# A hybrid decoder trunk on one core: the order of the long and the short product in the feed-forward blocks

## The chip, the cores and the metric

The kernel runs on one core of one Trainium2 chip. Its time is the device time of that core in microseconds (us), from launch to end; the profile's span is the time from the first to the last recorded instruction. The time before is 2571.78 us, the median of three runs (2567.96 to 2573.69).

## What is computed

Two layers of a decoder trunk over 256 tokens of width 2048, all in float32. Each layer has a modulation by a condition vector, head groups (gated DeltaNet and sliding-window attention) between an input and an output projection, and a SwiGLU feed-forward of inner width 5632. The change lies in the feed-forward alone:

```python
h = rms_norm(x, ln_ffn[l]) * (1.0 + sc_f) + sh_f
gate, up = jnp.split(h @ w_gate_up[l], 2, axis=-1)      # 2048 -> 2 x 5632
x = x + gt_f * ((jax.nn.silu(gate) * up) @ w_down[l])   # 5632 -> 2048
```

## The kernel before

The token axis is kept whole: an activation tile is 128 features by 256 tokens, and weights are the stationary operand of TensorE in blocks of 128x128. To keep float32 accuracy at the faster fp32r rate, each weight block w is split into a rounded part wh (a cast on ScalarE, ACT) and a remainder wl (a subtraction on VectorE, DVE, or in the projections partly on GpSimd, POOL). Each activation is split in the same way into a tile `a` of 128 x 2 x 256: `a[:, 0, :]` is the rounded part, written by ACT, and `a[:, 1, :]` the remainder, written by DVE. A product keeps three terms: wh with both parts of the activation, and wl with the rounded part.

In the projections (`mm3`) these are three products of 256 columns. In the feed-forwards (`mm2`, line 725) the two terms with wh are merged into one product of 512 columns, which fills a whole accumulation bank; the term with wl is a product of 256 columns onto the bank's first half. The two halves are added when the bank is emptied (`swiglu` for gate and up, `add_x` for down). A block is one weight block with one activation tile, so two products: here "long" for 512 columns, "short" for 256. Every product has a weight load of its own in the instruction stream.

Who calls `mm2`:
- `gemm_pair` (line 753): one gate block row and one up block row, 16 blocks each, into the two banks of one tile `pr`. 42 of the 44 pairs of a layer.
- `pair_quad` (line 779) through `quad`: the first two pairs of a layer, four accumulations side by side, because the activations are still being made (`make` in `normed`): for each k, four blocks go to four banks.
- `gemm_two` (line 746): the down projection, 22 blocks into one bank `psm`, for 16 output tiles and two halves of the inner width. The first eight of the 22 activations lie in a tile named `mid`, the rest in `act`.

In all, a layer has 44 x 2 x 16 = 1408 blocks of gate and up and 2 x 16 x 22 = 704 of down; with two layers 4224 blocks.

The order of everything is set while the program is recorded: a planner (`Steps`, `Timed`) keeps an estimated clock for each engine and lets small steps of other work, splits of coming weights (`Weights.split`, four blocks at a time) and transfers be issued between blocks (`S.tick()` in `into`, line 732). TensorE's estimate for a product depends on its form and columns. Transfers go out on one queue, that of SyncE (SP).

Of the kernel before, what the change touches and what calls it, by code (L numbers as in the profile page):

```python
# [26 lines left out]
D, T, L, H, NH, FT = 2048, 256, 2, 8, 16, 44  # L27
# [406 lines left out]
def trunk(tc, xT, bada, c, c_col, par, con, w_in, w_ba, w_ada0, w_ada, w_out, w_gu, w_dn, out):  # L434
    nc = Timed(tc.nc)
    with (
# [244 lines left out]
        first, na, nw = [], 0, 0  # L681
# [36 lines left out]
        def mm3(q, w, a, first, last):  # L718
# [3 lines left out]
            nc.tensor.matmul(q, wl, a[:, 0, :], start=False, stop=last)  # L722
            nc.floor = 0

        def mm2(q, w, a, first, last):

            wh, wl, nc.floor = w
            nc.tensor.matmul(q, wh, a.rearrange("p a c -> p (a c)"), start=first, stop=False)
            nc.tensor.matmul(q[:, 0:T], wl, a[:, 0, :], start=False, stop=last)
            nc.floor = 0  # L730

        def into(q, mm, acts, lo, hi):
# [13 lines left out]
        def gemm_two(acts, lo=0, hi=None, tag="pm"):  # L746

            S.grab(b, tag)
            q = b.bank(tag)
            into(q, mm2, acts, lo, len(acts) if hi is None else hi)  # L750
            return Held(q, lambda: b.give(tag))

        def gemm_pair(acts):

            S.grab(b, "pr")
            q = b.bank("pr")
            for i in range(2):
                into(q[:, i * 512 : i * 512 + 512], mm2, acts, 0, KT)
            return Held(q, lambda: b.give("pr"))
# [19 lines left out]
        def pair_quad(make):  # L779
            for _ in range(2):  # L780
                S.grab(b, "pr")
            qs = [Held(b.bank("pr"), lambda: b.give("pr")) for _ in range(2)]
            quad(mm2, [q.ap[:, i * 512 : i * 512 + 512] for q in qs for i in range(2)], make)
            return qs
# [960 lines left out]
```

## Time and profile before

| | |
|---|---|
| median of three runs | 2571.78 us (2567.96 to 2573.69) |
| the profiled execution's own time | 2571.36 us |
| its span | 2569.6 us |
| mean granted TensorE clock | 0.98 |
| products on TensorE (each with a load) | 16878 |
| HBM read | 603.44 MB |

How to read the profile: engines are PE (TensorE's products), PEld (its weight loads, which overlap PE), DVE, ACT, POOL and SP. A row of a group names line, engine, operation, the tiles (output <- inputs), shapes and count, then busy time in us, mean ns of one, and the engine's idle time just before with what ended it. Line 172 is the helper through which every operation is recorded, so groups are told apart by their tiles: `pr` is the accumulation of gate and up, `psm` that of down, of small work and of some projections, `pm` that of the projections. A row of the timeline is start, duration, engine, operation and tiles; PE's products overlap, since each begins while the one before it drains, so the distance between two starts is what a product costs, not its duration. Tile `act` or `mid` is the activation, `wh` and `wl` the weight's parts. PE's ends are modelled.

### The profile page before, as it was taken

What the parts mean: (1) busy time and instruction counts of PE and PEld (TensorE: products, weight loads), DVE (VectorE), ACT (ScalarE), POOL (GpSimd) and SP (SyncE); (2) the same over time, 40 slices, a digit from 0 to 9 for tenths busy, and PEclk for the clock granted to TensorE, in tenths of its full rate; (3) what the DMA queues carried; (4) which work ended last, traced back from release to release, by engine and by line L of the source; (5) the groups of instructions that cost most, each with busy time, mean ns of one, the idle gap of its engine ahead of it and who ended that gap; (6) DMA issues with size and microseconds to landing.
All of it is one profiled execution on the core that took longest, in us unless ns stands there. A gap on an engine that the chain in (4) does not pass through costs nothing.

```text
span 2569.6 us, 46036 instructions
## 1 busy us (share of the span) xinstructions
PE 2462.8 (96%) x16878; PEld 2174.5 (85%) x16878; DVE 1854.1 (72%) x3823; ACT 1294.3 (50%) x2760; POOL 432.7 (17%) x389
## 2 busy tenths in 40 slices
PE   6999898988999999999999999899899999999998
PEld 4887786987888888888888899899788888888887
DVE  3758767787667999999987876655877655555665
ACT  4346553535545445555445655454555544555553
POOL 1433232670000000000004333246000000000000
PEclk9999998998999999999999999899999999999999
DMA  9987575776777999999984443346677766555564
GB/s 353 338 302 255 194 244 181 249 272 199 244 245 268 341 354 347 352 345 344 328 299 132 133 131 126 118 161 225 214 253 246 243 187 191 189 183 195 180 185 137
DMA packets 192789, 609.08 MB, mean 237 GB/s; under 512 B 27825, under 2 KB 39217, under 8 KB 192561
## 3 DMA queue, kind: packets, MB, share of 16 engines
q1 hardware_dynamic: 192562, 606.14, 68.9%
q8 instruction: 132, 2.16, 0.3%
q14 instruction: 95, 0.78, 0.1%
HBM read 603.44 MB, written 2.10 MB: 236 GB/s over the span
## 4 chain that ended last, share of the span: by engine, by line
PE 52%; issue 32%; DVE 9%; DMA 3%; ACT 2%; POOL 1%; SPq 1%; DVEq 0%; POOLq 0%; ACTq 0%
PE psm L172 19%; PE pr L172 18%; PE pm L172 15%; DMA wada<-w_ada 3%; DVE wl L172 2%; ACT wh L172 1%; DVE wada L172 1%; POOL wl L172 1%; DVE act L172 1%; DVE cv L172 1%; DVE R L172 1%; DVE x L172 1%; DMA wx<-w_ada 0%; SPq L121 0%; DVE ry L172 0%
## 5 line engine op out<-in xcount | busy, mean ns | idle before, releaser
L172 ACT CAST wh<-w 128x512 fp32r<-128x512 f32 x1532 | 894.2, 604 | 456.7 <-PE psm L172 177.0
L172 DVE TENSOR_TENSOR wl<-w,wh 128x512 fp32r<-128x512 f32 (+1 forms) x1293 | 860.3, 683 | 243.7 <-ACT wh L172 234.4
L172 PE MATMUL pr<-act,wh 128*128 128x512 f32 x2816 | 994.7, 395 | 7.3 <-DVE kq L172 4.0
L172 PE MATMUL pr<-act,wl 128*128 128x256 f32 x2816 | 799.0, 284 | 0.0
L172 PE MATMUL pm<-act,wh 128*128 128x256 f32 x3328 | 641.4, 292 | 14.0 <-DVE x L172 4.1
L172 PEld LDWEIGHTS pr<-act,wh 128*128 128x128 f32 x2816 | 531.7, 189 | 132.3 <-DVE act L172 4.7
L172 PEld LDWEIGHTS pm<-act,wh 128*128 128x128 f32 x3328 | 519.0, 192 | 36.3 <-issue 21.2
L172 PEld LDWEIGHTS pr<-act,wl 128*128 128x128 f32 x2816 | 532.2, 189 | 0.0
L172 POOL TENSOR_TENSOR wl<-w,wh 128x512 fp32r<-128x512 f32 (+1 forms) x239 | 331.0, 1395 | 1190.9 <-PE psm L172 762.5
L172 PE MATMUL pm<-act,wl 128*128 128x256 f32 x1664 | 473.3, 284 | 1.4 <-POOL wl L172 1.4
L172 DVE CUSTOM_DVE_ANT_0 wada<-wada,cs 128x1024 f32<-128x1024 f32 x256 | 331.8, 1296 | 129.0 <-DMA wada<-w_ada 128.8
L172 PE MATMUL psm<-act,wh 128*128 128x512 f32 (+1 forms) x1280 | 390.8, 362 | 2.4 <-DVE act L172 2.1
L172 PEld LDWEIGHTS pm<-act,wl 128*128 128x128 f32 x1664 | 318.6, 191 | 2.3 <-POOL wl L172 2.2
L172 PE MATMUL psm<-act,wl 128*128 128x256 f32 x1088 | 308.3, 283 | 0.0
L172 PEld LDWEIGHTS psm<-act,wh 128*128 128x128 f32 x1280 | 228.3, 189 | 46.0 <-issue 6.1
L172 PEld LDWEIGHTS psm<-act,wl 128*128 128x128 f32 x1088 | 205.2, 189 | 0.0
L172 PE MATMUL psm<-mid,wh 128*128 128x512 f32 x512 | 183.4, 396 | 0.0
L172 PE MATMUL psm<-mid,wl 128*128 128x256 f32 x512 | 144.1, 281 | 0.0
L172 POOL TENSOR_TENSOR n2r<-ms,halfc 128x2 f32<-128x2 f32 x5 | 3.5, 690 | 803.5 <-DVE ms L172 803.5
L172 ACT COPY kq<-pr 128x512 f32<-128x512 f32 x88 | 51.6, 587 | 169.3 <-PE pr L172 169.1
L172 PEld LDWEIGHTS psm<-mid,wh 128*128 128x128 f32 x512 | 96.1, 188 | 22.8
L172 DVE TENSOR_TENSOR kq<-pr,kq 128x512 f32<-128x512 f32 x88 | 60.5, 687 | 72.9 <-ACT kq L172 72.9
(188 smaller groups left out, 1957.9 us busy)
## 6 DMA issues: line engine op xcount, KB each, us to landing
w<-w_gu SPq DMA_DIRECT2D x352, 512.0 KB
wada<-w_ada SPq DMA_DIRECT2D x320, 512.0 KB
w<-w_in SPq DMA_DIRECT2D x130, 512.0 KB
w<-w_dn SPq DMA_DIRECT2D x128, 512.0 KB
wx<-w_ada SPq DMA_DIRECT2D x64, 512.0 KB
w<-w_out SPq DMA_DIRECT2D x64, 512.0 KB
w<-w_dn SPq DMA_DIRECT2D x64, 384.0 KB
w<-w_in SPq DMA_DIRECT2D x28, 384.0 KB
```

Source lines behind the costliest of these rows:

```text
L172: return f(*a, **k)
```

## The change

A flag `turn` is kept across the calls of `mm2`. The first block of an accumulation sets it to 0; each later call flips it. Where it is 0 the block has the order of before, long then short. Where it is 1 the short product comes first. The flag that ends an accumulation is set on whichever product is last.

```diff
+        turn = [0]
+
         def mm2(q, w, a, first, last):
 
+
             wh, wl, nc.floor = w
-            nc.tensor.matmul(q, wh, a.rearrange("p a c -> p (a c)"), start=first, stop=False)
-            nc.tensor.matmul(q[:, 0:T], wl, a[:, 0, :], start=False, stop=last)
+            turn[0] = 0 if first else 1 - turn[0]
+            if turn[0]:
+                nc.tensor.matmul(q[:, 0:T], wl, a[:, 0, :], start=False, stop=False)
+            nc.tensor.matmul(q, wh, a.rearrange("p a c -> p (a c)"), start=first, stop=last and turn[0] > 0)
+            if not turn[0]:
+                nc.tensor.matmul(q[:, 0:T], wl, a[:, 0, :], start=False, stop=last)
             nc.floor = 0
```

On PE, in the middle of a gate-and-up accumulation of layer 0, these rows stood in a row before (output <- activation, weight part, columns last; numbers tell the buffers apart):

```order
L172 MATMUL pr_1996_8960<-act_1725_7765,wh_1985_8908 128x512
L172 MATMUL pr_1996_8960<-act_1725_7765,wl_1986_8909 128x256
L172 MATMUL pr_1996_8960<-act_1730_7784,wh_1985_8908 128x512
L172 MATMUL pr_1996_8960<-act_1730_7784,wl_1986_8909 128x256
L172 MATMUL pr_1996_8960<-act_1734_7801,wh_1985_8908 128x512
L172 MATMUL pr_1996_8960<-act_1734_7801,wl_1986_8909 128x256
L172 MATMUL pr_1996_8960<-act_1739_7820,wh_1985_8908 128x512
L172 MATMUL pr_1996_8960<-act_1739_7820,wl_1986_8909 128x256
```

and these stand there now:

```order
L172 MATMUL pr_1996_8960<-act_1725_7765,wh_1985_8908 128x512
L172 MATMUL pr_1996_8960<-act_1725_7765,wl_1986_8909 128x256
L172 MATMUL pr_1996_8960<-act_1730_7784,wl_1986_8909 128x256
L172 MATMUL pr_1996_8960<-act_1730_7784,wh_1985_8908 128x512
L172 MATMUL pr_1996_8960<-act_1734_7801,wh_1985_8908 128x512
L172 MATMUL pr_1996_8960<-act_1734_7801,wl_1986_8909 128x256
L172 MATMUL pr_1996_8960<-act_1739_7820,wl_1986_8909 128x256
L172 MATMUL pr_1996_8960<-act_1739_7820,wh_1985_8908 128x512
```

Long and short alternated; now two short ones and two long ones follow each other, with two different activations and, inside a pair, two different weight blocks of the same split.

On PE, at the end of one down accumulation and the beginning of the next, before:

```order
L172 MATMUL psm_3311_14781<-act_3258_14557,wh_3312_14784 128x512
L172 MATMUL psm_3311_14781<-act_3258_14557,wl_3313_14785 128x256
L172 MATMUL psm_3311_14781<-act_3285_14671,wh_3312_14784 128x512
L172 MATMUL psm_3311_14781<-act_3285_14671,wl_3313_14785 128x256
L172 MATMUL psm_3331_14869<-mid_2674_11995,wh_3315_14800 128x512
L172 MATMUL psm_3331_14869<-mid_2674_11995,wl_3316_14801 128x256
L172 MATMUL psm_3331_14869<-mid_2706_12135,wh_3315_14800 128x512
L172 MATMUL psm_3331_14869<-mid_2706_12135,wl_3316_14801 128x256
```

and now:

```order
L172 MATMUL psm_3311_14781<-act_3258_14557,wh_3312_14784 128x512
L172 MATMUL psm_3311_14781<-act_3258_14557,wl_3313_14785 128x256
L172 MATMUL psm_3311_14781<-act_3285_14671,wl_3313_14785 128x256
L172 MATMUL psm_3311_14781<-act_3285_14671,wh_3312_14784 128x512
L172 MATMUL psm_3331_14869<-mid_2674_11995,wh_3315_14800 128x512
L172 MATMUL psm_3331_14869<-mid_2674_11995,wl_3316_14801 128x256
L172 MATMUL psm_3331_14869<-mid_2706_12135,wl_3316_14801 128x256
L172 MATMUL psm_3331_14869<-mid_2706_12135,wh_3315_14800 128x512
```

Since a count of blocks is even and the first block keeps its order, an accumulation now ends with a long product and the next begins with one, so the pairs go on across the boundary, with the output tile changing inside a pair.

On PE, at the first units of a feed-forward (`pair_quad`), where four blocks share one activation that has just been made, the difference shows the waits (semaphores of the engine named) that the moved products carry:

```order
 L172 MATMUL pr_1707_7694<-act_1710_7699,wl_1690_7625 128x256
+L172 MATMUL pr_1706_7693<-act_1712_7712,wl_1680_7567 128x256 [waits Activation_49]
 L172 MATMUL pr_1706_7693<-act_1712_7712,wh_1679_7566 128x512 [waits DVE_49]
-L172 MATMUL pr_1706_7693<-act_1712_7712,wl_1680_7567 128x256
 L172 MATMUL pr_1706_7693<-act_1712_7712,wh_1682_7585 128x512
 L172 MATMUL pr_1706_7693<-act_1712_7712,wl_1683_7586 128x256
+L172 MATMUL pr_1707_7694<-act_1712_7712,wl_1688_7608 128x256
 L172 MATMUL pr_1707_7694<-act_1712_7712,wh_1687_7607 128x512
-L172 MATMUL pr_1707_7694<-act_1712_7712,wl_1688_7608 128x256
```

There the short product of the first block has moved ahead and waits for ACT alone, and the long one behind it waits for DVE as it did; of four blocks the first and the third have changed places of their products, so pairs arise here too.

## The prediction

> **What bounds the kernel now.** I read the page's busy shares and its chain first, then the chain in order of time inside the feed-forwards, then the sum by stretches, and last single products.
>
> ```profile
> span 2569.6 us, 46036 instructions
> PE 2462.8 (96%) x16878; PEld 2174.5 (85%) x16878; DVE 1854.1 (72%) x3823; ACT 1294.3 (50%) x2760; POOL 432.7 (17%) x389
> PE 52%; issue 32%; DVE 9%; DMA 3%; ACT 2%; POOL 1%; SPq 1%; DVEq 0%; POOLq 0%; ACTq 0%
> ```
>
> PE is busy for 96% of the span, so the question is what sets the spacing of its products. The chain names PE for 52% and "issue" for 32%; this "issue" is one stretch, and the windows show what it hides.
>
> ```profile
> 487.00 21.72 PE pm L172 x183
> 853.45 116.58 PE psm L172 x662
> 970.02 247.19 PE pr L172 x1408
> 1805.90 752.49 issue
> ...
> 970.00:1217.00 247.00, 247.00 (x1409) 216.44 (x1408) 225.61 (x427) 127.11 (x238) 0.00 (x0) 1.00 0.97 346
> 1814.00:2555.00 741.00, 738.99 (x4208) 647.09 (x4208) 476.51 (x841) 379.44 (x709) 0.00 (x0) 1.00 0.62 203
> ```
>
> A chain row is start, length, work. A window row is: stretch, length, busy time of PE, PEld, DVE, ACT and POOL with counts, granted clock, DMA share, GB/s. In layer 0 the chain runs over 1408 products without a step to another engine. The "issue" stretch is the feed-forward of layer 1: its window has PE busy 738.99 of 741.00 us with 4208 products, so it is the same dense stream. Spacing of products is therefore the whole bill: 247.19 / 1408 = 175.56 ns a product, 351.1 ns a block (one 512-column and one 256-column product), and 738.99 / 4208 = 175.6 in layer 1, the same. In the projections, where every product has 256 columns, 21.72 / 183 = 118.7 ns.
>
> How many blocks the change touches is in the groups by form:
>
> ```profile
> L172 PE MATMUL pr<-act,wh 128*128 128x512 f32 x2816 | 994.7, 395 | 7.3 <-DVE kq L172 4.0 <-DVE act L172 3.3
> L172 PE MATMUL psm<-act,wh 128*128 128x512 f32 x896 | 317.2, 393 | 1.9 <-DVE act L172 1.6 <-DVE mod L172 0.2
> L172 PE MATMUL psm<-mid,wh 128*128 128x512 f32 x512 | 183.4, 396 | 0.0
> ```
>
> 2816 + 896 + 512 = 4224 blocks, 4224 x 351.1 ns = 1483 us, 58% of the span. The mean durations (395 ns) are latencies that overlap, so I work with distances between starts:
>
> ```profile
> 1000.06 0.39 PE L172 MATMUL pr<-act,wh 128*128 128x512 f32 x1
> 1000.29 0.28 PE L172 MATMUL pr<-act,wl 128*128 128x256 f32 x1
> 1000.41 0.40 PE L172 MATMUL pr<-act,wh 128*128 128x512 f32 x1
> 1000.64 0.28 PE L172 MATMUL pr<-act,wl 128*128 128x256 f32 x1
> 1000.76 0.40 PE L172 MATMUL pr<-act,wh 128*128 128x512 f32 x1
> 1001.00 0.28 PE L172 MATMUL pr<-act,wl 128*128 128x256 f32 x1
> 1001.12 0.39 PE L172 MATMUL pr<-act,wh 128*128 128x512 f32 x1
> 1001.34 0.28 PE L172 MATMUL pr<-act,wl 128*128 128x256 f32 x1
> ...
> 1000.06 0.19 PEld L172 LDWEIGHTS pr<-act,wl 128*128 128x128 f32 x1
> 1000.29 0.19 PEld L172 LDWEIGHTS pr<-act,wh 128*128 128x128 f32 x1
> ```
>
> A 512-column product is followed after 0.23, 0.23, 0.24, 0.22 us, a 256-column one after 0.12 each time: 231 + 120 = 351. Each load starts with the product before its own, never earlier (the load for the product at 1000.29 stands at 1000.06).
>
> How much of 351 is the streaming of columns itself is seen where the clock is half:
>
> ```profile
> 591.29 0.80 PE L172 MATMUL pr<-act,wh 128*128 128x512 f32 x1 [1.64 <-DVE act L172]
> ...
> 592.10 0.63 PE L172 MATMUL pr<-act,wh 128*128 128x512 f32 x1
> 592.53 0.41 PE L172 MATMUL pr<-act,wl 128*128 128x256 f32 x1
> 592.74 0.63 PE L172 MATMUL pr<-act,wh 128*128 128x512 f32 x1
> ...
> 592.00:595.00 3.00, 3.00 (x11) 2.61 (x10) 3.00 (x8) 2.21 (x5) 0.00 (x0) 0.50 0.37 94
> ```
>
> At granted clock 0.50 a block takes 592.74 - 592.10 = 0.64 us, and its short product 0.21. Halved for the full clock: 320 ns a block and 107 a short product (an estimate from these rows). The measured 351 and 118.7 hold 31 ns and 12 ns more. If every product had the 12 ns of the 256-column streams, a block would have 24; so **7 ns a block** are left, and the question of the change is what they belong to.
>
> **The change part by part.** It removes nothing and adds nothing: 8448 products and as many loads, with the same operands, before and after; the other engines' rows stand in the same order, SP's transfers and POOL's among them. It moves the short product ahead of the long one in every other block. Counted over the two orders, neighbours of different length fall from 4224 + 4222 = 8446 to 2116 + 2116 = 4232; in their place stand 2106 pairs long-long and 2108 more pairs short-short. The terms:
>
> 1. *Short after short*, 2108 places. Nearest row: the projection stream, 118.7 ns, against the 120 that a short product takes in a block: -1.3 ns each, -2.8 us in all. But the 120 comes from rows rounded to 10 ns, and the split of 351 between its two products is worth less than their sum; the other end is 0. I take the middle, **-1.4 us**.
>
> The Trainium skill (TensorE: Matmul & The Clock Gate, section "LDWEIGHTS (loading the stationary operand)") gives a load as its columns over 1.2 GHz, so 107 ns for 128 columns, and its step "LDWEIGHTS" in Part 2 says that the next weights load while this product runs. By that rule a load nearly fills a short product whatever follows it; both kinds of neighbour would cost the same, and this term would be 0 where the row gives up to -2.8. The loads' starts above agree with one load under each product; how long the array is held by it no row shows, since the record's 0.19 us is longer than the 0.12 us pitch.
>
> 2. *Long after long*, 2106 places. The trace has no such pair. Bounds: the shortest distance after a long product in the rows above is 0.22 us, the longest 0.24, the mean 231 ns. At 0.22 it would save 11 ns x 2106 = 23 us, at 0.24 cost 9 x 2106 = 19 us. I take 231 ns, so **0**, because the distance after a long product varies between 0.22 and 0.24 though the follower is always the same short one: what varies there is not the follower's length. And by length alone the rows fit: fixed part f and slope s from f + 256 s = 118.7 and 2 f + 768 s = 351.1 give s = 0.444 ns a column and f = 5.0 ns; the halved cold rows give 0.417 a column. So a column costs 7% more at full clock than the halved slow clock says, in both streams, and nothing is left over for a change of length. In the cold rows a block costs just 3 x 0.21 us: there, a change of length costs nothing that can be seen.
>
> 3. *Waits.* In the first two units of each feed-forward, the first product at a new activation is now a short one, which reads only the rounded part (written by ACT), and the wait for the other part (DVE) falls one product later. That could save up to 0.12 us at 30 places, but only where PE waits there: the group above has 3.3 us of idle time behind "DVE act" in both layers together, and half of it, 1.64 us, stands ahead of the very first block of layer 0 (at 591.29), whose order is unchanged; the like number is left for layer 1's. 0. Elsewhere a piece of four blocks still begins with wh, so the first wait on ACT and the second on DVE stay at the same products; what is behind on PE's queue waits as before. 0.
>
> 4. *Cover.* DVE (225.61 of 247.00) and the transfers (share 0.97) in layer 0's second gate-up stretch lie just under PE. If PE went 1% quicker there, they would nearly be the bound; at the forecast nothing gets there.
>
> Sum: -1.4 us on the profiled execution's own 2571.36 us (span 2569.6 and 1.8 around it), 0.4 us under the median of 2571.78: **2570.0 us**. A measurement of this kernel can tell about 0.2% (5.1 us) from no change.
>
> **The rivals.** *Faster: the 7 ns belong to the change of length.* Each block has two changes, so 3.5 ns each (the 31.1 less 2 x 12 gives 7.1, half of it 3.55). The change takes away 8446 - 4232 = 4214 of them: -15 us, 2556.4 us. For it: the all-256 stream is really 7 ns a block cheaper than the mixed one by the fixed-cost reading, and the trace has no all-512 stream to deny it. Against it: the length reading in 2. explains the same two numbers, and the cold rows show no cost.
>
> *Slower: a worse cadence.* Starts fall into a repeated pattern, and the same two products have a second pattern in this trace, with other operands:
>
> ```profile
> 861.59 0.39 PE L172 MATMUL psm<-mid,wh 128*128 128x512 f32 x1
> ...
> 864.42 0.39 PE L172 MATMUL psm<-act,wh 128*128 128x512 f32 x1
> ...
> 869.33 0.39 PE L172 MATMUL psm<-mid,wh 128*128 128x512 f32 x1
> ```
>
> Eight blocks on mid take 2.83 us, 353.8 ns each; the next fourteen on act take 4.91 us, 350.7. Rounding makes this 1.5 to 4.6 ns; I take 2.5. If the new order holds the 3712 act blocks in the dearer pattern, it costs 2.5 x 3712 = +9.3 us: 2580.7 us. It decides from 5.1 us / 3712 = 1.4 ns a block. For it: the pattern plainly depends on more than lengths. Against it: one stretch of eight in twenty-two is all that shows it, and it returns to the cheaper one each time.
>
> *Slower: short products in a row starve the loads.* Two loads in succession then stand under short products. But in the projections every load does, over 183 products, at 118.7 ns; there is no adding up. I give it no chance of its own.
>
> *The change does nothing of what it says.* The order shows the pairs on PE; what remains is that a pair has no property of its own, which is the forecast.
>
> **How the numbers follow.** No change beyond terms 1 and 2: 0.47, with 2566 to 2575 as its own range. Lengths that cost by their changes, wholly or in part: 0.32, up to 2556. A dearer cadence or a long-long pair above 231 ns: 0.21, to 2581 and, at the bound of 0.24 us, to 2590. The range 2556 to 2581 leaves out the outer half of the bounds in term 2, some 1 in 6. Faster by over 0.2%: 0.32; within: 0.46; slower: 0.22.
>
> **What would show it.** In the after profile, the gate-up chain of 1408 products in layer 0 should last 247 us again (245 to 249). Starts two blocks apart should be 702 ns; a short product followed by a short one at 0.12, a long one followed by a long one at 0.23. If that last distance is 0.22 and the chain 244.7 us, the change of length was the cost; if it is 0.24 and the chain above 248.5, the cadence is. DVE's and ACT's counts per window must be as before. The forecast is wrong most simply if the distance after a long product does depend on what follows, which no row of before could show.

## The result, and the profile after

The changed kernel takes 2559.99 us (median of five runs, 2557.68 to 2562.28) against 2572.78 us (median of five, 2567.96 to 2580.23): ratio 0.995, 95% interval 0.9934 to 0.9966. That is 0.5% faster, 12.8 us between the medians. The forecast was 2570.0 us, no change that can be measured. The time lies inside the stated range of 2556 to 2581, but outside the forecast's own 2566 to 2575, and close to the faster rival's 2556.4.

The page of after, span and busy shares (the profiled execution itself took 2560.1 us):

```profile
span 2558.4 us, 45650 instructions
PE 2454.5 (96%) x16878; PEld 2166.9 (85%) x16878; DVE 1853.5 (72%) x3823; ACT 1295.8 (51%) x2760; POOL 433.7 (17%) x389
```

The span is 11.2 us shorter with the same products and loads, and PE is still busy for 96% of it. Two windows inside gate-up stretches, with the instructions on tile `pr` alone (the columns are stretch, length, then busy time and count of PE, PEld, DVE and ACT, granted clock, DMA share, GB/s); first before:

```profile
980.00:1200.00 220.00, 220.00 (x1255) 192.84 (x1254) 13.75 (x20) 11.74 (x20) 1.00 0.96 346
2200.00:2400.00 200.00, 200.00 (x1141) 175.28 (x1140) 12.45 (x18) 10.57 (x18) 1.00 0.57 190
```

and after:

```profile
980.00:1200.00 220.00, 220.00 (x1265) 192.55 (x1264) 13.07 (x19) 11.42 (x20) 1.00 0.97 347
2200.00:2400.00 200.00, 200.00 (x1150) 175.07 (x1149) 12.44 (x18) 9.98 (x17) 1.00 0.57 189
```

In the same 220 us there are 1265 products instead of 1255, in the same 200 us 1150 instead of 1141, at the same granted clock of 1.00. A block (two products) takes 2 x 220 / 1265 = 347.8 ns, not 350.6; counting whole products in a window blurs this by some 0.3 ns. PE is busy for all of both windows, before and after. So the gain is in the spacing of products, it is as large at a DMA share of 0.57 as at 0.97, and no wait is behind it.

Single products of after, PE's timeline (start, duration; neighbours of one kind are merged, x2):

```profile
1000.07 0.62 PE L172 MATMUL pr<-act,wh 128*128 128x512 f32 x2
1000.53 0.40 PE L172 MATMUL pr<-act,wl 128*128 128x256 f32 x2
1000.76 0.62 PE L172 MATMUL pr<-act,wh 128*128 128x512 f32 x2
1001.22 0.40 PE L172 MATMUL pr<-act,wl 128*128 128x256 f32 x2
1001.46 0.39 PE L172 MATMUL pr<-act,wh 128*128 128x512 f32 x1
```

Four blocks last 1001.46 - 1000.07 = 1.39 us. These rows are rounded to 10 ns; by the trace's starts in whole ns, four blocks take 1393 ns here, 348.3 each, and three blocks of before 1053 ns, 351.1 each. Two long products take 0.46 us, two short ones 0.23 or 0.24. In the down projection the 22 blocks of an output tile, eight on `mid` and fourteen on `act`, begin and end here:

```profile
865.70 0.39 PE L172 MATMUL psm<-mid,wh 128*128 128x512 f32 x1
...
868.48 0.39 PE L172 MATMUL psm<-act,wh 128*128 128x512 f32 x1
...
873.38 0.39 PE L172 MATMUL psm<-mid,wh 128*128 128x512 f32 x1
```

They take 7.68 us, before 7.74. The eight on `mid` went from 2.83 to 2.78 us, the fourteen on `act` from 4.91 to 4.90. The sum: 2816 blocks of gate and up at 2.8 ns less are 7.9 us, 64 output tiles of down at 0.06 us less 3.8 us, together 11.7 us against the 11.2 of the spans. The two feed-forwards together, each from the start of its first long product to that of its last, went from 1495.6 to 1485.9 us: 9.7 us, somewhat less than the 11.7, since single stalls of PE differ between the two executions.

### The profile page after: what moved, and what is told of

It is laid out like the page before. It is cut to its first block, busy times and chain, and to the rows that moved or that the text cites. A ratio compares the mean times of both kernels' runs of the same rounds, so it can differ in the third digit from the quotient of the medians.

```text
span 2558.4 us, 45650 instructions
## 1 busy us (share of the span) xinstructions
PE 2454.5 (96%) x16878; PEld 2166.9 (85%) x16878; DVE 1853.5 (72%) x3823; ACT 1295.8 (51%) x2760; POOL 433.7 (17%) x389
## 5 line engine op out<-in xcount | busy, mean ns | idle before, releaser
L172 PE MATMUL pr<-act,wh 128*128 128x512 f32 x2816 | 883.5, 394 | 7.6 <-DVE kq L172 4.4
L172 PE MATMUL pr<-act,wl 128*128 128x256 f32 x2816 | 561.6, 280 | 0.9 <-DVE wl L172 0.9
L172 PEld LDWEIGHTS pr<-act,wh 128*128 128x128 f32 x2816 | 433.5, 189 | 10.3 <-DVE kq L172 5.0
L172 PE MATMUL psm<-act,wh 128*128 128x512 f32 (+1 forms) x1280 | 363.8, 362 | 1.4 <-DVE act L172 1.2
L172 PE MATMUL psm<-act,wl 128*128 128x256 f32 x1088 | 233.3, 281 | 0.0
L172 PEld LDWEIGHTS psm<-act,wh 128*128 128x128 f32 x1280 | 201.4, 189 | 5.8 <-issue 3.7
L172 PE MATMUL psm<-mid,wh 128*128 128x512 f32 x512 | 169.7, 392 | 0.0
L172 PEld LDWEIGHTS psm<-mid,wl 128*128 128x128 f32 x512 | 96.1, 188 | 21.6
L172 DVE SCALAR_TENSOR_TENSOR x<-psm,mod,x 128x256 f32<-128x256 f32 x128 | 61.8, 483 | 57.4 <-PE psm L172 54.9
```

What stands on the lines that cost most here:

```text
L172: return f(*a, **k)
```

## The experiments

Three theories were left after the result. **Change of length**: each change from long to short or back costs 2.7 ns (351.1 less 348.4, the mean length of a block in the dense gate-up stretches of after, taken from the trace's starts). **Length reading**: a product costs by its own length, as the prediction had it, and something else makes the gain. **Cadence**: the starts fall into a repeated pattern that belongs to the order as a whole. To these come the operands (which product stands beside which) and the addresses of the tiles.

The table gives for each run the time, its ratio to the kernel before, and what 1408 gate-up products in a row took in the chain, per block; where the chain resolves no such stretch, the count in the 220 us window above. The kernel before has 247.19 us, 351.1 ns, and 1255.

| run | order of lengths | gate-up, per block | time, us | ratio, 95% interval |
|---|---|---|---|---|
| after | two and two | 1265 in 220 us | 2559.99 | 0.995 (0.9934 to 0.9966) |
| e1_runs4 | four and four | 247.18 us, 351.1 ns | 2566.38 | 0.9963 (0.9947 to 0.9978) |
| e2_long_only | long alone | 327.19 us, 232.4 ns a product | 3054.03 | |
| e3_shift | alternating, other neighbours | 247.29 us, 351.3 ns | 2574.16 | |
| e4_short_first | alternating, short first | 1255 in 220 us | 2568.64 | |
| e5_runs2 | two and two, other neighbours | 245.23 us, 348.3 ns | 2558.49 | |
| e6_before_shift32 | alternating, 32 bytes lower | 247.19 us, 351.1 ns | 2573.33 | 0.9993 (0.9979 to 1.0006) |
| e7_after_shift32 | two and two, 32 bytes lower | 1265 in 220 us | 2565.08 | 0.995 (0.9932 to 0.9968) |
| e8_before_shift64 | alternating, 64 bytes lower | 247.19 us, 351.1 ns | 2577.59 | |
| e9_runs2_timed | as e5 | 245.23 us, 348.3 ns | 2559.39 | 0.9944 (0.9927 to 0.9961) |
| e10_runs4_again | as e1 | 247.18 us, 351.1 ns | 2565.97 | 0.9968 (0.9955 to 0.9981) |
| e11_runs3 | three and three | 247.86 us, 352.1 ns | 2583.31 | |
| e12_other_half | alternating, other half of the bank | 247.19 us, 351.1 ns | 2578.97 | |

Times without an interval are single runs. Runs of the kernel before spread by 9 to 16 us within one group, so there the spacing in the trace decides. The kernel before stood between 2571.94 and 2576.55 us (medians) beside these groups.

**e1_runs4.** The short products of four blocks are kept back and issued together (in a down accumulation of 22 blocks the last group has two; `...` marks lines left out):

```diff
+        late = []
...
             nc.tensor.matmul(q, wh, a.rearrange("p a c -> p (a c)"), start=first, stop=False)
-            nc.tensor.matmul(q[:, 0:T], wl, a[:, 0, :], start=False, stop=last)
+            late.append((q, wl, a, nc.floor, last))
+            if last or len(late) == 4:
+                for q, wl, a, nc.floor, end in late:
+                    nc.tensor.matmul(q[:, 0:T], wl, a[:, 0, :], start=False, stop=end)
+                late.clear()
```

> The four long products of a split piece, then its four short ones (runs of four instead of two). Change-of-length theory (every change of length costs 2.7 ns, from 351.1 - 348.4 ns a block; a long and a short one without changes 345.7 together): half a change per block, 347.1 ns a block in the gate-up stretch, about 17 us under the kernel before, near 2555 us. Operand theory (what costs is that a short product follows or precedes the long one of its own block; half of the blocks still have that after the change, here none): 345.7 ns, near 2549 us. Cadence theory (the pattern of starts is a property of the whole order, no price per change): no reason to fall on 347.1; anything from 345 to 353 ns.

The chain of e1, inside the second gate-up stretch of layer 0 (start, length, products):

```profile
967.97 247.18 PE pr L172 x1408
```

A block takes 351.1 ns, as when lengths alternate, though there are a quarter of the changes. The change-of-length theory, which wanted 347.1, falls, and so does the operand theory's 345.7.

**e2_long_only.** `q[:, 0:T], wl, a[:, 0, :]` becomes `q, wl, a` with both parts, so all products have 512 columns (one more term than before is computed).

> The short product becomes a long one too (wl with both parts of the activation, a fourth term that the kernel leaves out), so the feed-forwards hold long products alone. Change-of-length theory: 345.7 - 118.7 = 227.0 ns from start to start. Length theory of the prediction (a product costs by its own length, 5.0 ns and 0.444 ns a column): 232.4 ns. Cadence theory: no forecast between 224 and 238. The kernel gets longer by some 430 to 480 us.

The chain and single products of e2:

```profile
1089.40 327.19 PE pr L172 x1408
...
1100.15 0.40 PE L172 MATMUL pr<-act,wl 128*128 128x512 f32 x1
1100.38 0.40 PE L172 MATMUL pr<-act,wh 128*128 128x512 f32 x1
1100.62 0.40 PE L172 MATMUL pr<-act,wl 128*128 128x512 f32 x1
1100.85 0.39 PE L172 MATMUL pr<-act,wh 128*128 128x512 f32 x1
```

327.19 / 1408 = 232.4 ns, the length reading's number to the digit, 5.4 above the other's 227.0. And 232.4 + 118.7 = 351.1, where 118.7 is the pure stream of the projections: on `act` tiles alternating costs the sum of the two pure streams. No price on a change of length is left in it. What has to be explained is why two and two costs less than the sum.

**e3_shift and e4_short_first.** In e3 each short product is issued one block later (`while len(late) > (0 if last else 1)`); in e4 the short one comes first in every block but an accumulation's first. In both, lengths alternate except for a pair at the ends of each accumulation.

> Each short product is put one block later (long k+1, short k, long k+2, ...): lengths alternate as before, but no short product stands beside the long one of its own block. Change-of-length theory: 351 ns a block as before (350.8 with the two pairs that each accumulation gets at its ends), about 2570 us. Operand theory: below 348.4 ns, 345.7 if the whole gain doubles, near 2549 us.

> The short product comes first in every block but the first of an accumulation: lengths alternate as before. Change-of-length theory: 350.8 ns a block, about 2570 us. If putting the short one first were the gain in itself, all blocks would have it: 345.7 ns, near 2549 us.

The chain of e3, then the window of e4:

```profile
968.85 247.29 PE pr L172 x1408
```

```profile
980.00:1200.00 220.00, 220.00 (x1255) 192.62 (x1255) 13.41 (x20) 11.17 (x19) 1.00 0.96 344
```

Both keep the spacing of before. Which block's short product stands beside a long one has no say, and putting it first is no gain in itself.

**e5_runs2.** e1 with `len(late) == 2`.

> Two long products, then their two short ones, then the next two long ones: the same sequence of lengths as the change (two and two), but other neighbours: a pair of short products uses the activations of the two long ones before it, and every accumulation ends with a short pair. If the sequence of lengths makes the gain: 348.4 ns a block in the gate-up stretches and 2560 us. If the neighbours make it: another number, 351 if the gain goes.

```profile
961.61 245.23 PE pr L172 x1408
...
980.00:1200.00 220.00, 220.00 (x1265) 192.56 (x1264) 13.78 (x20) 11.74 (x20) 1.00 0.98 351
```

The same 1265 products as after, and the chain gives them a better number: 348.3 ns a block. Other activations and weight parts follow each other here than in after. So the sequence of lengths, two and two, is what makes the gain.

The trace's starts, in whole ns, show what a pattern of starts is. In the dense gate-up stretches they repeat, to the 1 ns of the record: alternating, after every three blocks, 1053.3 ns, with distances of 224, 121, 235, 120, 233 and 120 ns; two and two (after and e5), after every four blocks, 1393.3 ns, with 224, 238, 117, 116, 231, 232, 116 and 120. The long products of e2 repeat after every seven, 1626.7 ns, in the stretch shown above. A long product's distance of 224 or 238 ns thus goes by its place in the cycle, and the whole cycle is what has a length. That is what the cadence theory says; why a sequence has the cycle it has, these runs do not show.

**e6, e7, e8: addresses.** The built program puts the `act` tiles at 544 bytes over a multiple of 2048, `mid` at 608. Since the two had different spacing in one stretch, all large tiles were moved down, by putting one-column constants together (in e8 into one more tile of constants, for 64 bytes); the edit of e6 and e7:

```diff
+        nws = b.t("nw", [128, L])
         for l in range(L):
-            t_ = b.t(f"nw{l}", [128, 1])
+            t_ = nws[:, l : l + 1]
```

> The kernel before, with all large tiles 32 bytes lower in each partition (two one-column constants share a tile); activations then start at a multiple of 64 bytes, before at 32 past one. Address theory (the pattern of starts comes from where the operands lie, as act and mid differ by 2 ns a block in the same stretch): another number than 351.1 (act, gate-up) and 352.8 (mid); if what costs is one more piece of 64 bytes for each product that starts off such a multiple, 16 columns at 0.417 ns for each product, 13 ns a block less, 338 ns, near 2515 us. Length theory without addresses: 351.1 again, 2572 us.

> The changed kernel with the same 32 bytes. Address theory: another number than 348.4 and 347.3 (mid), and if the extra piece is what costs, 335 to 338 ns, with the order of the products making no or another difference than 2.7 ns. Length-sequence theory: 348.4 again, 2560 us.

> The kernel before, with all large tiles 64 bytes lower: activations stand again at 32 past a multiple of 64, but act and mid change places in what is left of their addresses over 128 (act 32 to 96, mid 96 to 32). If the place over 128 decides: act 352.8 and mid 351 ns a block, the reverse of before, about 2578 us. If the place over 64 decides, or the tile has no say: 351.1 and 352.8 as before, 2572 us.

The windows of e6 and then e7:

```profile
980.00:1200.00 220.00, 220.00 (x1255) 192.80 (x1255) 13.77 (x20) 11.74 (x20) 1.00 0.97 346
```

```profile
980.00:1200.00 220.00, 220.00 (x1265) 192.55 (x1264) 13.76 (x20) 11.74 (x20) 1.00 0.96 348
```

Not one product more or less in this window than in before and in after. The chain of e8:

```profile
969.24 247.19 PE pr L172 x1408
```

The theory that addresses modulo 64 or 128 decide falls. The gain of the order stands at the new addresses too: e7 took 0.997 of e6's time (medians, 2565.08 and 2573.33 us); its 0.995 in the table is against the kernel before at the old addresses. Why `mid` blocks cost 2 ns more than `act` blocks in the order of before stays open.

**e9 and e10: the two orders timed.** e1's ratio of 0.9963 did not fit its spacing, so e5 and e1 were run again with five rounds.

> Two long, two short with the other neighbours, timed. If the sequence of lengths is all that counts: 348.4 ns a block again and the ratio of the change, 0.995. If the later use of the short product's weight part also saves waits (the order with runs of four was 0.9963 though its blocks took 351.1 ns): 348.4 ns and a lower ratio, 0.991 to 0.993.

> Runs of four again, to tell whether its 0.9963 stands and from where. If fewer stalls make it: 351.1 ns a block, and feed-forward stages that lose less than the 12 us of before to stalls. If its starts can fall in another pattern in another execution: a number below 351 ns in the gate-up stretch. If it was the spread of the runs: a ratio of 0.999 to 1.

e9 has the spacing of e5 and the ratio of the change, 0.9944 against 0.995, which their intervals do not tell apart. e10 has again the spacing of before, and again a gain, 0.9968. The chains of e9 and then e10:

```profile
972.61 245.23 PE pr L172 x1408
```

```profile
966.65 247.18 PE pr L172 x1408
```

The waits of PE on another engine inside layer 0's feed-forward (620 to 1335 us) and layer 1's (1840 to 2545), first in e6, whose order is that of before:

```profile
PE psm L172 <- DVE act L172: 3.6, 1, 3.6
PE psm L172 <- DVE mod L172: 0.2, 1, 0.2
...
PE pr L172 <- DVE wl L172: 1.7, 1, 1.7
```

and in e10, where this is the only row:

```profile
PE psm L172 <- DVE act L172: 0.4, 1, 0.4
```

With runs of four the weights' remainder `wl` is wanted after four long products instead of one, and the wait for it is not there in either profile of that order (e1's too has the one row of 0.4 us alone); for the first down block it waits 0.4 us instead of up to 3.6. In the six profiles where lengths alternate these waits add up to 1.3 us (e4) to 9.4 (e12, rows below), 1.8 in before; in two and two to between 1.7 (after) and 8.3 (e9). The length of the two feed-forwards, taken as above, agrees: 1494.1 and 1493.6 us in e1 and e10, 1494.9 to 1505.7 where lengths alternate, 1485.1 to 1495.0 in two and two. That speaks for a second, smaller gain of another kind, some 1 to 9 us in single executions. It was not shown to be all of the 0.3%, since only the profiled executions show waits; nor that the later use of `wl` is its cause, since three long products are 0.7 us and single waits for `wl` lasted up to 2.6.

**e11_runs3 and e12_other_half.** e1 with `len(late) == 3`; and the order of before, with the short product of every second block added onto the bank's second half (`q[:, half[0] * T : half[0] * T + T]`).

> Three long, three short. Length reading: 351.1 ns a block. If only the sequence of two and two has the cheaper pattern: 351.1. If odd runs are as good as pairs: 348.4 or lower.

> The order of before, but the short product of every second block adds onto the second half of the bank instead of the first. If the gain of the pairs came from which part of the bank follows which: another number than 351.1 ns a block. If the sequence of lengths sets the pattern: 351.1, 2572 us.

The chain of e11:

```profile
975.35 247.86 PE pr L172 x1408
```

The chain of e12, and its waits in layers 0 and 1:

```profile
966.12 247.19 PE pr L172 x1408
...
PE psm L172 <- DVE act L172: 2.9, 1, 2.9
PE psm L172 <- DVE mod L172: 0.2, 1, 0.2
...
PE pr L172 <- DVE wl L172: 6.3, 5, 2.6
```

Three and three takes 352.1 ns, a little more than the sum of the streams; its profiled execution, the only one, also lost 12 us to waits for DVE in the two feed-forwards. The half of the bank has no say (247.19 us); e12's longer time fits the 9.4 us of waits in its profiled execution, against 1.8 in that of before. Two and two is the only order tried that goes below 351 ns in gate and up, by 2.8 ns, and it does so with both neighbours and at both addresses tried, in both layers.

## Where the prediction held and where it failed, by its own steps

That the time lies in the stated range is luck: the range's lower end came from the faster rival, and the forecast, no change, is off by 10.0 us, where the interval of the ratio ends at 0.9966.

**What bounds the kernel** held: the spacing of products is the bill, and the gain is 4224 blocks times a few ns. **The length reading** of term 2, that a product costs 5.0 ns and 0.444 ns a column, held for long products alone, 232.4 ns, and for lengths that alternate; it does not hold in two and two. **The faster rival** came near the time with a mechanism that the runs refute: with a price on each change (3.5 ns, or 2.7 after the result) e1 should have gained again in its spacing, and at 2.7 e2 should have shown 227.0.

**The step that failed** is the sum of terms 1 and 2. I priced each new pair at a distance that a product has in another order, 231 ns for long after long and 118.7 to 120 for short after short, and left the distances from long to short and from short to long as they were. In after all of them differ. The means in the window from 980 to 1200 us, from the trace's starts:

| distance, ns | before | after |
|---|---|---|
| long to short | 230.6 | 234.6 |
| long to long | | 227.5 |
| short to long | 120.6 | 118.3 |
| short to short | | 116.3 |

Two blocks take 696.7 ns where the terms gave 702.2 - 0.7. Behind the two long products they take about 1 ns more than before, so term 2's nothing comes out nearly right as a sum, though neither of its distances stayed at 231. Behind the two short products they take about 6.5 ns less, where term 1 had 0.7. The bounds for a long product, 0.22 to 0.24 us, were not crossed. The lower bound of term 1 was: 116.3 ns is below the 118.7 that I took for the lowest. I read the 0.22 and 0.24 us after a long product as a sign that followers do not count; they are places in a cycle of three blocks, and another order has another cycle. I had the right kind of mechanism in the rival of a second pattern of starts and looked at it in one direction only: I had seen a dearer one (`mid`) and gave a cheaper one no chance. The direction of a pattern that no row shows was not known.

**Term 1** (short after short, -1.4 us) had the right sign and was too small in gate and up. In down, short pairs took 118.7 ns on `act` and 119.2 on `mid`, inside its bounds, so no one price of a short pair gives the whole gain. **Waits** (term 3, nothing) stood: the waits above are 1.8 us in the profile of before and 1.7 in that of after. **Cover** (term 4) stood too: at a DMA share of 0.97 the stretch still gained its 2.8 ns. The rival in which short products in a row **starve the loads** was rightly given nothing: two in a row cost less than before.

**The signs I named** were not sharp enough: the gate-up chain at 244.7 us was to mean the change of length. e5's chain is 245.23, the distance from long to long 227.5 ns, and these alone would have confirmed a false cause; it took e1 and e2 to part them.

## What to carry to other kernels

Where PE is dense, the order of products of different lengths was worth some tenths of a per cent here, and it did not follow from prices per product or per change: measure the few orders that do the same work by the length of a dense stretch in the trace, which repeats to 0.1% where the times spread by 0.5%. Before a fitted price is believed, test it on the pure stream that it predicts; one run of long products alone parted two readings that had agreed on everything seen until then. An order that wants an operand later can also pay by waits that vanish; two and two with its short products kept back by four blocks might join both effects, and was not run.

## What the runs showed of the hardware that was not expected

- At a granted clock of 1.00 a 512-column fp32r product with a load of its own takes 232.4 ns in a pure stream (e2), a 256-column one 118.7 (the projections of before), and the two alternating on `act` 351.1, their sum. The Trainium skill (TensorE: Matmul & The Clock Gate, section "Back-to-back issue gap") gives columns over 2.4 GHz and 2.5 ns for the gap of a product by itself, an estimate of 215.8 and 109.2 ns, and for a stream of loads and products a shorter one, about 131 ns at 512 columns. The measured distances in these fp32r streams are 8 to 9% longer than the first, and no run comes near the second.
- In gate and up, on `act`, two and two costs 348.3 ns a block, three and three 352.1, four and four 351.1, alternating 351.1. Other neighbours (e3, e5) and addresses 32 bytes lower (e6, e7) changed neither alternating nor two and two; 64 bytes (e8) and the other half of the accumulation bank (e12) were run for alternating alone. The starts repeat exactly, alternating after 1053.3 ns and two and two after 1393.3. What in the engine makes the pattern of two and two shorter is not settled.
- In the down projection eight blocks on `mid` took 2.83 us before and 2.78 after, while those on `act` barely moved (4.91 and 4.90 us for fourteen): the same order is worth 5.4 ns a block on the one and 1.2 on the other. The place modulo 128 bytes is not the reason: in e8, where the two change places in it, both keep their spacing (2.82 and 4.91 us by the trace's starts).
